# Two gate quads of the second token half: from plain filling of the second attention to Strassen quads behind the first half's

## The chip, the cores and the metric

One core of a Trainium2 chip runs the whole kernel. The metric is device microseconds of one execution; before the change the median of three runs is 2586.55 us.

## The reference, cut to what matters

One encoder layer on 2048 tokens of width 1024, in float32.

```python
h = rms_norm(x, norm_mix)
z = h @ w_in        # q_A 512 | k_A 128 | v_A 128 | q_B 512 | k_B 512 | v_B 512 | gate_A 1024 | gate_B 1024
y_a = windowed_gqa(q_a, k_a, v_a, sink)          # |t - s| <= 128
y_b = neighborhood_attn(q_b, k_b, v_b, rpb)      # on the 32 x 64 token grid
gates = sigmoid(concat([g_a, g_b]) + b_gate)
merged = gates[..., :1024] * (y_a @ w_proj_a) + gates[..., 1024:] * (y_b @ w_proj_b)
x = x + merged @ w_out
h2 = rms_norm(x, norm_mlp)
x = x + square(relu(h2 @ w_up)) @ w_down
out = rms_norm(x, norm_final)
```

The change concerns `z = h @ w_in` alone, and of it the 1024 columns of gate_B for tokens 1024 to 2047.

## The kernel before, in words

Every product of float32 operands is made of three matmuls: an operand is split into a high part (a cast on ScalarE, `L314`) and a low part (what the cast left, a subtraction on VectorE, `L315`), and high x high, high x low and low x high are added up in PSUM (`mm3s`, L318 to L320, or `mm3`, L205 to L207).

Tokens are four blocks of 512. The first two blocks ("the first half") are projected in **quads**. A quad is a 2 x 2 Strassen-Winograd product: two blocks of 256 columns of `w_in`, two halves of the 1024 features, two token blocks. Seven products instead of eight, in the order 1, 2, 5, 6, 7, 4, 3 (`ORDER`); each has two tiles of 128 columns, each tile 4 chunks x 3 matmuls of 128x512. A quad has a left operand for each product, made from its weights (`zraw`, two loads of 1 MB, then sums on VectorE and splits into `zwhl`, a ring of three buffers), and a right operand, a **page** of h (`zh1` to `zh7`, high and low part), which is the same for all quads. Three PSUM banks for each tile column, x, z and y, take products 1 and 2, 5 and 3, and 6, 7 and 4; between products VectorE adds what a bank holds to a partial result (`zc`, L309), and the next product into that bank waits for that. There are nine quads: one for k_A and v_A, one for q_A, three for q_B, k_B, v_B, four for the gates. I count them from one: the sixth to the ninth make the gates. Gate results go to DRAM (`zg`) by SP's queue.

The third and fourth block ("the second half") are normalised during the sixth and seventh quad and written to DRAM as `h1d`. Behind the ninth quad they are loaded again, multiplied by the gain `g_mix` and split into `hT` (`h_pages`, L703 to L716). Their projection is **plain**: slices of 128 columns (`raw`, 512 KB, split into `whl` by ScalarE and POOL), 8 chunks x 3 matmuls for each of the two blocks. These tiles are the filling of the two attentions: `fill` gives one chunk, three matmuls, at a time, and `plain(upto)` takes as many as a formula says between an attention's scores, transposes and products. The first attention takes 192 chunks (`PLAIN`). The second has 32 units of 4 steps, and spreads over its 128 steps the chunks up to 520 (`last_plain + PLAIN`). The last 24 are issued at its end. The order of the tiles is: k_A, v_A, q_A, then k_B, q_B, v_B by turns, then the 16 gate tiles (`gate_tile`).

In a step of the second attention (`turn`, `score`, `plain`, `product`) TensorE transposes the weights of one unit into `pt`, scores a unit two further on into `s`, does filling, and multiplies the transposes of the step before with `vb`. VectorE adds the bias to scores (L1114), ScalarE takes the exponential (L1122), POOL scales (L1127) and makes bias tiles from `braw` (L1064).

Source order is a priority; a scheduler that knows a time model of the chip sets the order on each engine, and an engine then works its instructions in that order.

Of the kernel before, what the change touches and what calls it, by code (L numbers as in the profile page):

```python
# [8 lines left out]
F32 = mybir.dt.float32  # L9
F32R = mybir.dt.float32r  # L10
AF = mybir.ActivationFunctionType
ALU = mybir.AluOpType
# [3 lines left out]
D = 1024  # L16
# [79 lines left out]
def encoder_layer(ctx, tc, x, norm_mix, w_in, b_gate, sink, rpb, w_pa, w_pb, w_out,  # L96
# [295 lines left out]
    def in_weights(c, w):  # L392

        return [row_half(c, w, p) for p in range(2)]
# [83 lines left out]
    def is_v(col):  # L478
        return col == O_VA or O_VB <= col < O_GA

    def in_result(col, b, src, in_psum):

        if col < O_VB and col != O_VA:
            for dst, t in qk_parts(col, b, src, in_e()):
                SY.dma_start(dst, t)
            return
        if in_psum:
            t = in_e()[:, 0] if is_v(col) else in_c()
            A.copy(t, src)
            src = t  # L490
        if is_v(col):
            for dst, t in v_parts(col, b, src, zbank(tpool, 2), in_v2[-1]()):
                SY.dma_start(dst, t)
        else:
            f = (col - O_GA) // P
            SY.dma_start(zg[b][0][f // 8, (f % 8) * P : (f % 8 + 1) * P, :], src)

    def in_quad(c, w, lf, right, ybanks=ypool, zbanks=zpool):

# [160 lines left out]
            G.tensor_scalar(tb, tb, 8.0, 1.0, ALU.mult, ALU.mult)  # L660
            SY.dma_start(tabs[n], tb)

    for q in range(2, len(QUADS)):
        if q == 5:
            s_v.close()
            in_v2.pop()
# [5 lines left out]
        if q + 1 < len(QUADS):  # L672
            ws = in_weights(*QUADS[q + 1])
        if q in (5, 6):

            b = q - 3
# [4 lines left out]
        for n, _ in enumerate(quad2 if q == 2 else in_quad(*QUADS[q], iter(lf), right)):  # L681
# [1158 lines left out]
```

## Time and profile before

| what | value |
|---|---|
| runs | 2582.53, 2586.55, 2589.74 us |
| profiled execution, span from first to last instruction | 2581.8 us |
| TensorE busy, granted clock | 2557.6 us (99%), 0.999 |
| VectorE, ScalarE, POOL busy | 1607.1, 1235.7, 404.0 us |
| ninth quad | 318.84 to 357.66 us of the span |
| first attention | from there to about 609 us |
| second attention | about 609 to 993 us |

A matmul's busy time overlaps with the next one's, so TensorE's 99% says that it hardly ever waits, not that it is at its peak. The profiled execution's own time is its span; nothing else is known of it, and it lies 4.75 us under the median of the runs.

### The profile page before, as it was taken

What the parts mean: (1) busy time and instruction counts of PE and PEld (TensorE: products, weight loads), DVE (VectorE), ACT (ScalarE), POOL (GpSimd) and SP (SyncE); (2) the same over time, 40 slices, a digit from 0 to 9 for tenths busy, and PEclk for the clock granted to TensorE, in tenths of its full rate; (3) what the DMA queues carried; (4) which work ended last, traced back from release to release, by engine and by line L of the source; (5) the groups of instructions that cost most, each with busy time, mean ns of one, the idle gap of its engine ahead of it and who ended that gap; (6) DMA issues with size and microseconds to landing.
All of it is one profiled execution on the core that took longest, in us unless ns stands there. A gap on an engine that the chain in (4) does not pass through costs nothing.

```text
span 2581.8 us, 34876 instructions
## 1 busy us (share of the span) xinstructions
PE 2557.6 (99%) x12200; PEld 2142.3 (83%) x12200; DVE 1607.1 (62%) x2617; ACT 1235.7 (48%) x2265; POOL 404.0 (16%) x630
## 2 busy tenths in 40 slices
PE   8999999999999999999999999999999999999999
PEld 6888888888888888888888888888888888888887
DVE  8866657765544445566578767866665535554766
ACT  5334357775555555443335554554454322323454
POOL 1001126665555440000000000100000000000010
PEclk9999999999999999999999999999999999999999
DMA  5657496577867647675357656844428835444555
GB/s 183 204 159 208 131 270 167 128 197 188 221 198 203 186 131 238 221 220 179 124 170 241 231 210 209 305 162 166 148 110 311 280 102 184 142 154 160 187 195 172
DMA packets 354128, 490.41 MB, mean 190 GB/s; under 512 B 28808, under 2 KB 188808, under 8 KB 351776
## 3 DMA queue, kind: packets, MB, share of 16 engines
q1 hardware_dynamic: 346896, 471.14, 58.5%
q10 hardware_dynamic: 7056, 17.04, 1.8%
q8 instruction: 96, 1.57, 0.3%
q14 instruction: 80, 0.66, 0.1%
HBM read 328.64 MB, written 159.45 MB: 189 GB/s over the span
## 4 chain that ended last, share of the span: by engine, by line
PE 89%; DVE 3%; DMA 3%; ACT 1%; issue 1%; POOL 1%; SPq 1%; POOLq 0%; ACTq 0%; DVEq 0%
PE b L318 15%; PE b L320 15%; PE b L319 15%; PE mm L207 5%; PE mm L205 5%; PE mm L206 5%; PE zb L320 3%; PE zb L318 3%; PE zb L319 3%; PE pt L205 2%; PE pt L206 2%; PE pt L207 2%; PE av L1159 2%; PE pt L1138 2%; PE s L1107 2%; PE av L920 1%
## 5 line engine op out<-in xcount | busy, mean ns | idle before, releaser
L319 PE MATMUL b<-dwh,dah 128*128 128x512 f32 x896 | 348.5, 389 | 0.0
L320 PE MATMUL b<-dwh,dah 128*128 128x512 f32 x896 | 347.6, 389 | 0.0
L318 PE MATMUL b<-dwh,dah 128*128 128x512 f32 x896 | 339.6, 389 | 0.0
L314 ACT CAST dah<-da 128x1024 fp32r<-128x1024 f32 (+1 forms) x128 | 120.9, 945 | 368.2 <-PE b L320 242.7
L315 DVE TENSOR_TENSOR dah<-da,dah 128x1024 fp32r<-128x1024 f32 (+1 forms) x128 | 139.5, 1090 | 223.7 <-ACT dah L314 220.7
L319 PE MATMUL b<-ubh,uwhlb 128*128 128x512 f32 x592 | 230.3, 389 | 0.0
L318 PE MATMUL b<-ubh,uwhlb 128*128 128x512 f32 x592 | 230.2, 389 | 0.0
L320 PE MATMUL b<-ubh,uwhlb 128*128 128x512 f32 x592 | 229.2, 389 | 0.0
L205 PE MATMUL mm<-hT,whl 128*128 128x512 f32 x544 | 218.4, 402 | 0.0
L207 PE MATMUL mm<-hT,whl 128*128 128x512 f32 x544 | 213.6, 393 | 0.0
L206 PE MATMUL mm<-hT,whl 128*128 128x512 f32 x544 | 213.1, 392 | 0.0
L319 PEld LDWEIGHTS b<-dwh,dah 128*128 128x128 f32 x896 | 168.2, 188 | 34.9
L320 PEld LDWEIGHTS b<-dwh,dah 128*128 128x128 f32 x896 | 168.2, 188 | 34.9
L318 PEld LDWEIGHTS b<-dwh,dah 128*128 128x128 f32 x896 | 168.2, 188 | 34.9
L318 PE MATMUL zb<-zh,zwhl 128*128 128x512 f32 x476 | 186.7, 394 | 5.2 <-DVE zh L542 1.6
L319 PE MATMUL zb<-zh,zwhl 128*128 128x512 f32 x476 | 186.3, 391 | 0.0
L320 PE MATMUL zb<-zh,zwhl 128*128 128x512 f32 x476 | 183.6, 392 | 0.3 <-DVE zwhl L315 0.3
L309 DVE TENSOR_TENSOR uc<-b,uc 128x512 f32<-128x512 f32 x160 | 109.1, 689 | 103.1 <-PE b L320 102.0
L1710 POOL TENSOR_TENSOR st<-st,power 128x1 f32<-128x1 f32 x16 | 13.3, 841 | 925.1 <-DVE st L1709 925.1
L318 PEld LDWEIGHTS b<-ubh,uwhlb 128*128 128x128 f32 x592 | 111.1, 188 | 23.4 <-issue 0.4
L319 PEld LDWEIGHTS b<-ubh,uwhlb 128*128 128x128 f32 x592 | 111.1, 188 | 23.2
L320 PEld LDWEIGHTS b<-ubh,uwhlb 128*128 128x128 f32 x592 | 111.1, 188 | 23.1
(272 smaller groups left out, 5883.8 us busy)
## 6 DMA issues: line engine op xcount, KB each, us to landing
at<-uc SPq DMA_DIRECT2D x224, 256.0 KB
da<-at SPq DMA_DIRECT2D x96, 512.0 KB
dw<-in_w_down_dram SPq DMA_DIRECT2D x160, 256.0 KB
uraw<-in_w_up_dram SPq DMA_DIRECT2D x32, 1024.0 KB
raw<-in_w_in_dram SPq DMA_DIRECT2D x34, 512.0 KB
zraw<-in_w_in_dram SPq DMA_DIRECT2D x16, 1024.0 KB
z<-zg SPq DMA_DIRECT2D x64, 256.0 KB
zg<-zc SPq DMA_DIRECT2D x32, 256.0 KB
```

What stands on the lines that cost most here:

```text
L205: PE.matmul(ps, lh, rh, start=first, stop=False)
L206: PE.matmul(ps, lh, rl, start=False, stop=False)
L207: return PE.matmul(ps, ll, rh, start=False, stop=last).ins
L309: return eng.tensor_tensor(out=out, in0=a, in1=b, op=op).ins
L314: casts.append(A.copy(hi, src).ins)
L315: return eng.tensor_tensor(out=lo, in0=src, in1=hi.bitcast(F32), op=ALU.subtract).ins
L318: PE.matmul(ps, lh, rh, start=first, stop=False, skip_group_check=True)
L319: PE.matmul(ps, lh, rl, start=False, stop=False, skip_group_check=True)
L320: PE.matmul(ps, ll, rh, start=False, stop=last, skip_group_check=True)
L1107: ins = PE.matmul(ps[:, :n], self.q[:, i, :], kv[:, z, B_R0[i] // 4 : (B_R0[i] + B_NR[i]) // 4, 4 * B_C0[j] : 4 * (B_C0[j] + w)], start=z ...
L1138: ins = PE.transpose(pt[:kp, at + (i - i0) * P : at + (i - i0 + 1) * P], self.s[i][:, rr : rr + kp], ident).ins
L1159: ins = PE.matmul(po[:, i0 * P : (i0 + ni) * P], self.v[:kp, c, :], src[:kp, o : o + ni * P], start=pair == x == z == 0, stop=(c == 7 and ...
```

## The change

The third and fourth gate quad (the 1024 columns of gate_B) are made for the second half too, as Strassen quads ten and eleven, behind the ninth. Their pages replace those of the first half in the same buffers (`late_page`): while the ninth quad runs, each page is built as soon as its product there is over, from `h1d`. Pages 1, 2 and 3 are blocks: two loads into the low part's place, then the gain by ScalarE (high part) and by VectorE (low part, `SCALAR_TENSOR_TENSOR` L680). Pages 5 and 7 are differences of two blocks, pages 6 and 4 those of a block and an earlier page (its high and low part, one after the other); they are loaded by halves of 512 KB into `xin`, a ring of three. The eight gate tiles of these columns leave the filling, so that 8 gate tiles are left, and `last_plain` becomes 25 x 8 chunks in place of 41 x 8: the second attention spreads 200 chunks over its 128 steps, before 328.

```diff
@@ in_result, a gate result's place
-            SY.dma_start(zg[b][0][f // 8, (f % 8) * P : (f % 8 + 1) * P, :], src)
+            SY.dma_start(zg[first_block[0] + b][0][f // 8, (f % 8) * P : (f % 8 + 1) * P, :], src)
...
-    for q in range(2, len(QUADS)):
+    LATE = QUADS[7:]
+
+    def late_page(n):
+
+        hi, lo = in_page[n](), in_page[n]()
+        j, p = {1: (0, 0), 2: (0, 1), 3: (1, 1), 5: (1, 0), 6: (1, 1), 7: (1, 1), 4: (0, 1)}[n]
+        gains = [g_mix[:, p * 4 + k : p * 4 + k + 1] for k in range(4)]
...
+        def parts(src, h, l, at):
+            for k in range(2):
+                A.activation(h[:, k], src[:, k], AF.Copy, scale=gains[at + k])
+                V.scalar_tensor_tensor(out=l[:, k], in0=src[:, k], scalar=gains[at + k], in1=h[:, k].bitcast(F32),
+                                       op0=ALU.mult, op1=ALU.subtract)
+
+        def half_page(z, j, p):
+            t = T(xp, [P, D], F32, "xin", 3).rearrange("p (k c) -> p k c", k=2)
+            SY.dma_start(t, rows(j, p, z))
+            return t
+
+        if n < 4:
+            for z in range(2):
+                SY.dma_start(halves(lo)[z].bitcast(F32), rows(j, p, z))
+        for z, (h, l) in enumerate(zip(halves(hi), halves(lo))):
+            if n < 4:
+                parts(l.bitcast(F32), h, l, 2 * z)
+                continue
+            a = half_page(z, j, p)
+            if n == 5:
+                b = half_page(z, 0, 0)
+                add(V, a, a, b, ALU.subtract)
+                parts(a, h, l, 2 * z)
+                continue
+            for k in range(2):
+                A.activation(a[:, k], a[:, k], AF.Copy, scale=gains[2 * z + k])
+            if n == 7:
+                b = half_page(z, 1, 0)
+                for k in range(2):
+                    A.activation(b[:, k], b[:, k], AF.Copy, scale=g_mix[:, 2 * z + k : 2 * z + k + 1])
+                add(V, a, a, b, ALU.subtract)
+            else:
+                for t in late[{6: 5, 4: 6}[n]]:
+                    add(V, a, a, halves(t)[z].bitcast(F32), ALU.subtract)
+            split(a, h, l, V)
+        late[n] = hi, lo
+
+    late = {}
+    plan = [(c, w, 0) for c, w in QUADS] + [(c, w, 2) for c, w in LATE]
+    for q in range(2, len(plan)):
...
+        first_block[0] = plan[q][2]
+        if q == len(QUADS):
+            right = late
+        for n, _ in enumerate(quad2 if q == 2 else in_quad(*plan[q][:2], iter(lf), right)):
+            if q == len(QUADS) - 1:
+                late_page(ORDER[n])
...
-    dense += [gate_tile(f, (2, 3)) for f in range(16)]
+    GATES = [f for f in range(16) if all(not c <= O_GA + f * P < c + 2 * w for c, w in LATE)]
+    dense += [gate_tile(f, (2, 3)) for f in GATES]
...
-    scored, begin, SCORE, last_plain = 0, given, 0.4, 41 * KC
+    scored, begin, SCORE, last_plain = 0, given, 0.4, (9 + 2 * len(GATES)) * KC
```

What it moves is seen at three places. The first is VectorE in the ninth quad, from the split of product 6's weights to the addition of the second tile's product 6 (`zc<-zb,zc`). Before, with the page work for the first attention (`hT`) between:

```order
L315 TENSOR_TENSOR zwhl_2616<-zS_2614,zwhl_2616 128x1024
L714 SCALAR_TENSOR_TENSOR hT_2937<-raw_2938,g_mix,hT_2936 128x512 x2
L714 SCALAR_TENSOR_TENSOR hT_2937<-raw_2944,g_mix,hT_2936 128x512 x2
L315 TENSOR_TENSOR zwhl_2619<-zraw_2394,zwhl_2619 128x1024
L714 SCALAR_TENSOR_TENSOR hT_2951<-raw_2952,g_mix,hT_2950 128x512 x2
L714 SCALAR_TENSOR_TENSOR hT_2951<-raw_2958,g_mix,hT_2950 128x512 x2
L309 TENSOR_TENSOR zc_2728<-zb_2715,zc_2642 128x512
L315 TENSOR_TENSOR zwhl_2622<-zraw_2396,zwhl_2622 128x1024
L182 TENSOR_TENSOR whl_3011<-raw_3009,whl_3011 128x1024
L309 TENSOR_TENSOR zc_2743<-zb_2730,zc_2657 128x512
```

The same place now, with pages 1, 5, 6 (in `xin`) and 2 of the second half:

```order
L315 TENSOR_TENSOR zwhl_2616<-zS_2614,zwhl_2616 128x1024
L309 TENSOR_TENSOR zS_2965<-zraw_2631,zraw_2629 128x1024
L680 SCALAR_TENSOR_TENSOR zh_279_2664<-zh_279_2664,g_mix,zh_278_2663 128x512 x4
L315 TENSOR_TENSOR zwhl_2619<-zraw_2394,zwhl_2619 128x1024
L680 SCALAR_TENSOR_TENSOR zh_285_2744<-xin_2745,g_mix,zh_284_2743 128x512 x2
L309 TENSOR_TENSOR xin_2795<-xin_2795,zh_284_2743 128x1024
L680 SCALAR_TENSOR_TENSOR zh_285_2744<-xin_2754,g_mix,zh_284_2743 128x512 x2
L309 TENSOR_TENSOR zc_2776<-zb_2763,zc_2646 128x512
L309 TENSOR_TENSOR xin_2795<-xin_2795,zh_285_2744 128x1024
L315 TENSOR_TENSOR zwhl_2622<-zraw_2396,zwhl_2622 128x1024
L680 SCALAR_TENSOR_TENSOR zh_283_2706<-zh_283_2706,g_mix,zh_282_2705 128x512 x2
L309 TENSOR_TENSOR zc_2791<-zb_2778,zc_2661 128x512
```

Between the two additions now stand a subtraction, a split and a gain pair, before two splits; ahead of the first stands page 5, which needs product 5 to be over.

The second place is SP's queue at the start of the ninth quad, from the last gate writes of the eighth on. Before, the loads for the first attention come behind them:

```order
L496 DMA zg_100<-zc_2512 128x512
L710 DMA raw_2938<-h1d_97 128x2x512
L710 DMA raw_2944<-h1d_97 128x2x512
L710 DMA raw_2952<-h1d_97 128x2x512
L496 DMA zg_99<-zc_2671 128x512
```

Now pages 1 and 2 (`zh`), the next weights (`zraw`) and the halves of pages 6 and 7 (`xin`):

```order
L498 DMA zg_100<-zc_2512 128x512
L690 DMA zh_279_2664<-h1d_97 128x2x512 x2
L498 DMA zg_99<-zc_2687 128x512
L690 DMA zh_283_2706<-h1d_97 128x2x512 x2
L498 DMA zg_99<-zc_2702 128x512
L552 DMA zraw_2980<-in_w_in_dram 128x4x512
L685 DMA xin_2803<-h1d_98 128x2x512
L685 DMA xin_2845<-h1d_98 128x2x512
L552 DMA zraw_2982<-in_w_in_dram 128x4x512
L685 DMA xin_2849<-h1d_98 128x2x512
```

Each of these waits in its place for a buffer to come free, and what follows waits with it.

The third place is TensorE in the second attention, one step from a score (`s`) to the products (`av`) that follow it. Before, two chunks of filling stand there, three in other steps:

```order
L1107 MATMUL s_10270<-kb_1137_9456,qb_1236_10130 128x384 x2
L205 MATMUL mm_10239<-hT_3016,whl_9917 128x512
L206 MATMUL mm_10239<-hT_3017,whl_9917 128x512
L207 MATMUL mm_10239<-hT_3016,whl_9917 128x512
L205 MATMUL mm_10239<-hT_3030,whl_9917 128x512
L206 MATMUL mm_10239<-hT_3031,whl_9917 128x512
L207 MATMUL mm_10239<-hT_3030,whl_9917 128x512
L1159 MATMUL av_666_10184<-phb_10220,vb_1202_9893 128x256
```

Now one chunk, two in other steps:

```order
L1166 MATMUL s_10366<-kb_1180_9709,qb_1254_10185 128x512 x2
L205 MATMUL mm_10371<-hT_3602,whl_9905 128x512
L206 MATMUL mm_10371<-hT_3603,whl_9905 128x512
L207 MATMUL mm_10371<-hT_3602,whl_9905 128x512
L1218 MATMUL av_664_10352<-phb_10334,vb_1242_10098 128x256
```

A third or more of the filling between a score and the products is gone. At the end of the ninth quad TensorE's order also has four matmuls of the tenth's product 1 between products 7 and 4.

More of the change, by code (lines that the diff above doesn't have):

```diff
@@ L479, in is_v @@
         return col == O_VA or O_VB <= col < O_GA
+    first_block = [0]
     def in_result(col, b, src, in_psum):
@@ L661, in bias_tables, with rows @@
             SY.dma_start(tabs[n], tb)
-    for q in range(2, len(QUADS)):
+    LATE = QUADS[7:]
[3 more added lines that the diff above has]
+        gains = [g_mix[:, p * 4 + k : p * 4 + k + 1] for k in range(4)]
+        def rows(j, p, z):
+            r = p * BT + z * 256
+            return h1d[j][r : r + 256, :].rearrange("(k p) t -> p k t", p=P)
+        def parts(src, h, l, at):
[35 more added lines that the diff above has]
+    for q in range(2, len(plan)):
         if q == 5:
@@ L671, in encoder_layer @@
         lf = list(in_left(ws, 256, (1, 2) if q == 2 else ()))
-        if q + 1 < len(QUADS):
-            ws = in_weights(*QUADS[q + 1])
+        if q + 1 < len(plan):
+            ws = in_weights(*plan[q + 1][:2])
         if q in (5, 6):
@@ L680, in encoder_layer @@
         ops2.extend(lf if q == 2 else ())
-        for n, _ in enumerate(quad2 if q == 2 else in_quad(*QUADS[q], iter(lf), right)):
+        first_block[0] = plan[q][2]
[4 more added lines that the diff above has]
+                late_page(ORDER[n])
             if q == 6 and n == 0:
```

## The prediction

> **What bounds the kernel now.** I read the page first, then the busy times of the stages, then the timeline and the waits where the change acts.
>
> ```profile
> PE 2557.6 (99%) x12200; PEld 2142.3 (83%) x12200; DVE 1607.1 (62%) x2617; ACT 1235.7 (48%) x2265; POOL 404.0 (16%) x630
> ...
> L205 PE MATMUL mm<-hT,whl 128*128 128x512 f32 x544 | 218.4, 402 | 0.0
> ...
> L318 PE MATMUL zb<-zh,zwhl 128*128 128x512 f32 x476 | 186.7, 394 | 5.2 <-DVE zh L542 1.6
> ```
>
> TensorE is the bound over the whole span, so a matmul less is time less, unless TensorE then waits. A matmul's own 390 to 400 ns are no price, since matmuls overlap; the price is the step from start to start. The stages (the eighth quad, the ninth, the first attention, the second):
>
> ```profile
> 281.00:319.00 38.00, 38.00 (x169) 31.49 (x168) 20.39 (x23) 9.52 (x11) 4.96 (x6) 1.00 0.27 86
> 319.00:357.50 38.50, 38.02 (x169) 31.11 (x167) 25.72 (x34) 19.48 (x27) 3.01 (x26) 1.00 0.75 229
> 357.50:609.00 251.50, 249.50 (x1482) 216.88 (x1480) 167.43 (x490) 178.52 (x506) 156.42 (x322) 1.00 0.65 175
> 609.00:993.00 384.00, 383.01 (x2218) 337.05 (x2219) 178.94 (x448) 216.75 (x505) 188.56 (x204) 1.00 0.69 190
> ```
>
> Columns: stretch, its length, busy time of PE, PEld, DVE, ACT, POOL, granted clock, DMA share, GB/s. TensorE idles 0, 0.5, 2.0 and 1.0 us in them. In quads VectorE does the rest of the work (20.4 of 38 us), in the second attention ScalarE (56%).
>
> The profiled span, 2581.8 us, is 4.75 us under the median of 2586.55 and just under the fastest of the three runs (2582.53). Everything below is a difference inside this span, and is put on the median.
>
> **The change, part by part.**
>
> *Matmuls taken away.* Eight gate tiles leave the filling: 8 x 2 blocks x 8 chunks x 3 = 384 matmuls. Their step there is read from nine filling matmuls between a score and a product:
>
> ```profile
> 783.78 0.39 PE L205 MATMUL mm<-hT,whl 128*128 128x512 f32 x1
> ...
> 785.83 0.28 PE L1159 MATMUL av<-phb,vb 128*128 128x256 f32 x1
> ```
>
> 2.05 us for nine, 0.228 each: 384 x 0.228 = 87.5 us less in the second attention.
>
> *Matmuls added.* Two quads of 7 products x 2 tiles x 4 chunks x 3 = 168 matmuls. The rows are the ninth quad's start and the starts of its product 6 (twelve matmuls for each of two tiles), that product's second tile, product 7, its second tile, and product 4:
>
> ```profile
> 318.84 0.39 PE L318 MATMUL zb<-zh,zwhl 128*128 128x512 f32 x1
> ...
> 335.16 0.39 PE L318 MATMUL zb<-zh,zwhl 128*128 128x512 f32 x1
> 337.88 0.39 PE L318 MATMUL zb<-zh,zwhl 128*128 128x512 f32 x1
> 340.60 0.39 PE L318 MATMUL zb<-zh,zwhl 128*128 128x512 f32 x1
> 343.32 0.39 PE L318 MATMUL zb<-zh,zwhl 128*128 128x512 f32 x1
> 346.68 0.47 PE L318 MATMUL zb<-zh,zwhl 128*128 128x512 f32 x1 [0.47 <-DVE zc L309]
> ```
>
> Twelve take 2.72 us, 0.2267 each: a quad takes 38.1 us, two take 76.2. Net of both: -11.3 us.
>
> *Pages of the second token half.* This is new vector work in front of TensorE, and the last row above already shows its danger: product 4 started 0.64 us late (346.68 for 343.32 + 2.72), because its bank was still to be read by a VectorE addition that stood behind page work. VectorE's rows there, from the last addition of the eighth quad on:
>
> ```profile
> 319.69 0.68 DVE L309 TENSOR_TENSOR zc<-zb,zc 128x512 f32<-128x512 f32 x1
> ...
> 335.55 2.74 DVE L714 SCALAR_TENSOR_TENSOR hT<-raw,g_mix,hT 128x512 fp32r<-128x512 f32 x4
> 338.20 0.69 DVE L309 TENSOR_TENSOR zc<-zb,zc 128x512 f32<-128x512 f32 x1
> 338.80 1.22 DVE L315 TENSOR_TENSOR zwhl<-zraw,zwhl 128x1024 fp32r<-128x1024 f32 x1
> 339.93 1.22 DVE L182 TENSOR_TENSOR whl<-raw,whl 128x1024 fp32r<-128x1024 f32 x1
> ...
> 344.52 1.41 DVE L714 SCALAR_TENSOR_TENSOR hT<-raw,g_mix,hT 128x512 fp32r<-128x512 f32 x2
> 345.84 0.69 DVE L309 TENSOR_TENSOR zc<-zb,zc 128x512 f32<-128x512 f32 x1
> 346.44 0.75 DVE L714 SCALAR_TENSOR_TENSOR hT<-raw,g_mix,hT 128x512 fp32r<-128x512 f32 x1
> ```
>
> From start to start a 128x1024 operation costs 1.14 us (338.80 to 339.93), a 128x512 addition 0.60, a pair with the gain 1.32. The seven pages need 16 gain operations (10.6 us) and 18 of 128x1024 (20.5 us; two of them stand in the eighth quad): 31 us of VectorE. ScalarE gets 32 activations of 128x512 (0.64, by the row of four in 2.58 below) and 6 casts of 1.05: 27 us, which its 9.5 us in a quad leave room for. VectorE has 17.6 us free in a quad, so it must borrow from the tenth quad too. I follow the order of the new program with these steps, the ninth quad starting at 318.84 as now:
> - Page 5 can be written when product 5 has been read, at 335.16. ScalarE (0.65) and VectorE's pair, subtraction and second pair end at 339.95; the addition that frees product 6's first bank ends at 340.6, when product 7 wants it: 0.2 us.
> - A subtraction, a weight split and page 2's first pair (3.6 us) stand ahead of the addition for the second bank: it ends at 344.75, TensorE was there at 343.5: 1.35 us.
> - Four matmuls of the tenth quad's product 1 now stand ahead of product 4. Their weights are cast when product 7 gives its buffer back (its second tile now ends at 344.9 + 2.7 = 347.6), 1.05 us and two handovers: 1.35 us.
> - Up to the additions after product 6 of the tenth quad VectorE has 33 operations of 1024, 16 with the gain and 10 additions, 54 us, from 320.3 on, and its own waits (for freed pages, loads, casts), 8 to 10.5 us as I step through them: the end is at 382.5 to 385. TensorE is there at 318.84 + 38.1 + 21.8 (four products) + 2.9 (the waits above) = 381.6: 1.0 to 3.4 us.
>
> The sum is 3.9 to 6.3 us; the two ends are loads that land in 3 or in 5.1 us. The row that bounds the load: a 512 KB load issued at 333.48 was waited for until 338.57; one issued at 332.15 was used unwaited by the row of 334.75.
>
> ```profile
> 332.15 0.36 SPq L710 DMA_DIRECT2D raw<-h1d  x1
> 333.48 0.38 SPq L192 DMA_DIRECT2D raw<-in_w_in_dram  x1
> ...
> 334.75 2.58 ACT L713 ACTIVATE hT<-raw,g_mix 128x512 fp32r<-128x512 f32 x4
> 337.24 1.04 ACT L314 CAST zwhl<-zraw 128x1024 fp32r<-128x1024 f32 x1
> 338.57 1.05 ACT L181 CAST whl<-raw 128x1024 fp32r<-128x1024 f32 x1 [0.29 <-DMA raw<-in_w_in_dram]
> ```
>
> I take +5. From below the bound is 0 (all hidden, 17.6 us free in each quad); from above 31 - 17.6 = 13.5 us, if only the ninth quad's room served. The 0.64 us of today comes from the page work for the first attention, which follows the last quad in either kernel, and stays. The Trainium skill, "DMA: Bandwidth & Descriptors", section "Bandwidth", measures 6.15 us for a load of 1 MB; by that, an estimate, page 2 would be whole about 0.7 us later than I have it and the sum that much worse.
>
> *DMA and queues.* 18 loads of 512 KB for pages, four of 1 MB for weights, and 16 gate writes of 256 KB that SP now issues (the ACT queue did). SP passes them in order: behind page 2's load stand gate writes and the next weights, and one weight load waits there for its buffer until about 347, with a page 7 load behind it. That one is used some 6 us after it lands, so it costs nothing unless the landing slips by that much. The stretch 281 to 319 moves 86 GB/s, so the engines have room.
>
> *The second attention with half its filling.* It shrinks from 384 to about 296.5 us, each of its 128 steps from 3.0 to 2.3 us. ScalarE loses 8 casts of 1.05 and 16 copies of 0.58, POOL 8 splits of 2.40: their busy shares become 67%, VectorE's 60%, POOL's 57%. The first attention runs at 71%, 67% and 62% and idles TensorE 2.0 us in 251.5. At that rate 296.5 us would idle 2.4 instead of 1.0: +1.4 at most by this row, 0 at least; I take +0.9. The upper bound is from the one load that came late:
>
> ```profile
> 653.99 3.06 POOL L1064 TENSOR_TENSOR biass<-braw,masks 128x288 f32<-128x288 f32 x3 [13.56 <-DMA braw<-tab]
> ...
> 657.59 0.88 PE L1138 MATMUL pt<-ident,sb 128*96 128x128 f32 x3 [0.20 <-POOL sb L1127]
> ```
>
> POOL stood 13.56 us, scaling the scores stood behind it, and TensorE lost 0.2 us there. Scores are made five steps ahead of their transposes, 15 us now and 11.6 then: the same lateness would cost 3.4 us more, twice that for two such loads, +7.
>
> *Sum.* -11.3 + 5 + 0.9 = -5.4 us: 2586.55 - 5.4 = 2581.2 us.
>
> **Rivals.**
>
> 1. *The pages hide wholly.* VectorE has 17.6 us free in each quad and TensorE's order could absorb the rest. Against it speaks the 0.64 us that 13 us of such work cost already. Then -11.3 + 0.9, 2576.2 us.
>
> 2. *A stall trips the clock.* Here TensorE idled 1.57 and 0.34 us within 3 us, and then ran eight matmuls in 3.5 us at a granted clock of 0.53 (the third column from the end of the stretch):
>
> ```profile
> 52.24 0.47 PE L318 MATMUL zb<-zh,zwhl 128*128 128x512 f32 x1 [1.57 <-DVE zh L542]
> ...
> 53.27 0.79 PE L320 MATMUL zb<-zh,zwhl 128*128 128x512 f32 x1 [0.34 <-DVE zwhl L315]
> ```
>
> ```profile
> 53.00:56.50 3.50, 3.23 (x8) 2.55 (x9) 3.50 (x5) 0.29 (x1) 0.00 (x0) 0.53 0.00 0
> ```
>
> Nearly half of 3.5 us is lost, 1.7 us a time. The waits above of 1.35 us lie 4 us apart, near that; two trips give 2584.6 us. The Trainium skill, "TensorE: Matmul & The Clock Gate", Part 1, says that the clock halves after an idle window of about 3.4 us. By that rule none of these waits would trip it and the sum stays; this trace disagrees, with 1.9 us of idleness.
>
> 3. *Slower: the DMA engines bind the second attention's first half.* The loads of keys, queries, values and bias come per step, and steps get 23% shorter, while the q, k, v filling of the first 16 units is still there.
>
> ```profile
> 609.00:660.00 51.00, 50.01 (x284) 43.28 (x285) 26.22 (x63) 28.91 (x66) 25.05 (x27) 1.00 0.86 221
> 660.00:710.00 50.00, 50.00 (x296) 44.20 (x295) 26.45 (x64) 29.46 (x68) 27.40 (x32) 1.00 0.89 238
> ...
> 640.00:660.00 20.00, 19.67 (x111) 16.90 (x110) 9.19 (x25) 11.37 (x29) 6.44 (x9) 1.00 0.80 170
> ```
>
> By tile sizes 16 units move some 24.6 MB and six q, k, v tiles 9.4 MB, 34 MB in 148 us: 230 GB/s. Full engines would give 221/0.86 = 257 or 267 GB/s, so it fits; at the rate of 640 to 660 (170/0.80 = 212) it takes 160 us, 12 us more: 2592 us. It turns the sign from 220 GB/s downward (34 MB in 154 us).
>
> That fewer matmuls were not issued is no rival: two quads of 168 against 384 is a count.
>
> **How the numbers follow.** The forecast (2579 to 2584) gets 0.43, hidden pages (2574 to 2579) 0.33, clock trips or the upper ends of both stalls (2584 to 2588) 0.15, the DMA case 0.09. About 0.3%, 7.8 us, is what a measurement of this kernel can tell from no change: faster than 2578.8 are the hidden pages and a little of the forecast, 0.36; slower than 2594.3 is the far half of the DMA case with longer stalls, 0.06; the rest 0.58. The range of 8 in 10 reaches from 2574 (-12.5: pages hidden and the waits of the attention gone) to 2590.
>
> **What would show it.** Right: 48 matmuls fewer; the second attention near 296 us with TensorE idle under 3 us; two quads more of 38 us, in which TensorE waits 4 to 6 us in all, for zc additions (L309) and for zwhl casts, at product 7 and ahead of product 4. Wrong: TensorE idle under 2 us in the ninth and tenth quad; or POOL waiting for braw and TensorE for POOL in the second attention; or a granted clock under 1.0 near 345 to 385 us. The largest doubt is the tenth quad, where VectorE's lateness is a sum of many handovers that no row of before shows.

## The result and the profile after

The changed kernel takes 2602.16 us (median of 4 runs, 2598.18 to 2604.14) against 2585.91 for the kernel before: a ratio of 1.0063, interval 1.0048 to 1.0077. It is slower by 16 us; 2581.2 was forecast. The profiled execution, the fastest of the four, has a span of 2596.4 us, 14.6 more than that of before.

The engines' line of the page shows the count of the forecast, 48 matmuls fewer, and TensorE at 98%:

```profile
PE 2554.7 (98%) x12152; PEld 2138.5 (82%) x12152; DVE 1676.8 (65%) x2693; ACT 1262.5 (49%) x2301; POOL 384.8 (15%) x622
```

The stages after (eighth, ninth, tenth, eleventh quad; first attention; second; the stretch behind it; the rest), in the columns of the prediction's windows (length, busy PE, PEld, DVE, ACT, POOL, granted clock, DMA share, GB/s):

```profile
280.50:322.50 42.00, 39.94 (x169) 32.63 (x168) 23.43 (x25) 10.64 (x13) 4.59 (x6) 0.96 0.57 191
322.50:363.50 41.00, 38.76 (x170) 31.34 (x169) 35.01 (x40) 23.59 (x32) 0.00 (x0) 1.00 0.56 198
363.50:405.40 41.90, 39.98 (x170) 32.61 (x169) 32.40 (x36) 19.40 (x26) 0.00 (x0) 0.96 0.34 121
405.40:445.00 39.60, 38.33 (x170) 31.43 (x169) 25.98 (x34) 19.48 (x27) 3.41 (x27) 1.00 0.73 233
445.00:696.60 251.60, 249.15 (x1480) 216.60 (x1479) 167.52 (x489) 178.49 (x506) 156.11 (x321) 1.00 0.65 174
696.60:1007.80 311.20, 301.52 (x1844) 268.42 (x1845) 178.20 (x448) 198.69 (x479) 169.34 (x196) 0.99 0.77 207
1007.80:1021.60 13.80, 11.04 (x51) 9.07 (x50) 3.91 (x5) 6.13 (x11) 0.00 (x0) 1.00 0.47 143
1021.60:2596.40 1574.80, 1567.93 (x6914) 1297.35 (x6913) 999.64 (x1336) 679.16 (x1021) 34.72 (x33) 1.00 0.57 194
```

The account by starts of stages in the two traces:

| stage | before | after | count alone | excess |
|---|---|---|---|---|
| up to the first attention's filling | 357.7 | 445.0 (+87.3) | +76.2 | +11.1 |
| first attention | 251.3 | 251.6 (+0.3) | 0 | +0.3 |
| second attention and the filling behind it | 397.2 | 325.0 (-72.2) | -87.5 | +15.3 |
| the rest | 1575.6 | 1574.8 (-0.8) | 0 | -0.8 |

The sum of the last column is 25.9; with -11.3 from the counts it gives +14.6. So the counts hold, and both stages that were given small terms (+5 and +0.9) lost far more. What TensorE waited for, first in the quads, then from the second attention on (total, times, longest; one of the five waits for `zc`, 0.5 us, lies ahead of the eighth quad):

```profile
PE zb L318 <- DVE zc L309: 6.8, 5, 2.1
PE zb L318 <- ACT zwhl L314: 1.1, 1, 1.1
...
PE pt L1197 <- POOL sb L1186: 5.7, 1, 5.7
PE mm L205 <- ACT z L1010: 2.8, 1, 2.8
PE av L1218 <- DVE plb L1205: 1.9, 5, 0.6
PE s L1166 <- DVE stb L1173: 1.7, 2, 0.9
```

The single waits, from TensorE's timeline:

```profile
288.62 0.50 PE L318 MATMUL zb<-zh,zwhl 128*128 128x512 f32 x1 [2.06 <-DVE zc L309]
348.31 0.50 PE L318 MATMUL zb<-zh,zwhl 128*128 128x512 f32 x1 [1.11 <-DVE zc L309]
352.46 0.50 PE L318 MATMUL zb<-zh,zwhl 128*128 128x512 f32 x1 [1.13 <-ACT zwhl L314]
387.32 0.47 PE L318 MATMUL zb<-zh,zwhl 128*128 128x512 f32 x1 [1.93 <-DVE zc L309]
434.00 0.47 PE L318 MATMUL zb<-zh,zwhl 128*128 128x512 f32 x1 [1.27 <-DVE zc L309]
704.98 0.50 PE L1166 MATMUL s<-kb,qb 128*128 128x512 f32 x1 [0.83 <-DVE stb L1173]
741.84 0.66 PE L1197 MATMUL pt<-ident,sb 128*96 128x128 f32 x2 [5.71 <-POOL sb L1186]
1010.86 0.50 PE L205 MATMUL mm<-hT,whl 128*128 128x512 f32 x1 [2.76 <-ACT z L1010]
```

Three of them bring half clock, at which half of TensorE's busy time is lost: 1.7 us in each of the first two rows, 2.4 in the third, where TensorE was busy for 4.76 of the 6.8 us (the third column from the end is the granted clock):

```profile
289.20:292.70 3.50, 3.50 (x10) 2.75 (x9) 3.43 (x4) 0.00 (x0) 1.60 (x2) 0.51 0.88 263
388.20:391.70 3.50, 3.50 (x10) 2.72 (x9) 1.84 (x2) 0.00 (x0) 0.00 (x0) 0.51 0.00 0
739.80:746.60 6.80, 4.76 (x16) 3.86 (x17) 0.66 (x3) 0.48 (x1) 5.80 (x10) 0.50 0.81 239
```

Taken from start to start, less the usual step, the quads' five waits cost 2.22, 1.27, 1.30, 2.09 and 1.44 us, 8.3 in all; with 3.4 us at half clock and less the 0.64 us of before that is the 11.1. From 696.6 to 1021.6 us the waits that cost over 0.34 us each sum to 13.0 (before: 0.8); with the 2.4 at half clock that is 14.6 more than before, about the 15.3 of the table.

The wait at 741.84 has its beginning on POOL:

```profile
738.34 2.97 POOL L1123 TENSOR_TENSOR biass<-braw,masks 128x288 f32<-128x288 f32 x3 [9.44 <-DMA braw<-tab]
741.28 2.10 POOL L1186 TENSOR_SCALAR sb<-sb,stb 128x288 f32<-128x288 f32 x4
```

POOL stood 9.4 us for one bias load, the scaling of the scores stood behind it, and TensorE behind that. Of the DMA engines at that time:

```profile
705.00:717.00 12.00, 10.67 (x61) 8.99 (x62) 8.10 (x20) 6.26 (x15) 4.45 (x6) 1.00 1.02 276
717.00:729.00 12.00, 12.00 (x76) 10.84 (x75) 7.71 (x20) 9.73 (x25) 8.78 (x8) 1.00 1.07 277
729.00:738.30 9.30, 7.13 (x46) 6.23 (x44) 5.65 (x13) 5.63 (x15) 0.00 (x0) 1.00 1.08 228
```

They are full (share above 1) for 33 us, at 228 to 277 GB/s. The kernel before has such a stretch at the same place, 32 us long:

```profile
619.00:629.00 10.00, 9.34 (x54) 8.22 (x54) 6.39 (x17) 5.16 (x14) 3.54 (x5) 1.00 1.04 285
629.00:640.00 11.00, 11.00 (x67) 9.80 (x66) 6.89 (x16) 7.55 (x17) 8.31 (x8) 1.00 1.06 314
640.00:651.00 11.00, 11.00 (x64) 9.64 (x63) 5.58 (x16) 6.68 (x16) 0.42 (x1) 1.00 1.08 206
```

So the engines had no room there before the change either. Steps of 3.0 us left the loads their time, and TensorE idled 0.7 us in these rows; shorter steps ask for the same loads sooner (ramp, below, tests that).

### The profile page after: what moved, and what is told of

It is laid out like the page before. It is cut to its first block, busy times and chain, and to the rows that moved or that the text cites. A ratio compares the mean times of both kernels' runs of the same rounds, so it can differ in the third digit from the quotient of the medians.

```text
span 2596.4 us, 34955 instructions
## 1 busy us (share of the span) xinstructions
PE 2554.7 (98%) x12152; PEld 2138.5 (82%) x12152; DVE 1676.8 (65%) x2693; ACT 1262.5 (49%) x2301; POOL 384.8 (15%) x622
## 4 chain that ended last, share of the span: by engine, by line
PE 83%; DVE 2%; DMA 2%; ACT 1%; issue 1%; POOL 1%; SPq 0%; POOLq 0%; DVEq 0%; ACTq 0%
PE b L318 16%; PE b L319 16%; PE b L320 16%; PE mm L205 4%; PE mm L207 4%; PE mm L206 4%; PE pt L205 2%; PE pt L206 2%; PE pt L207 2%; PE av L1218 2%; PE pt L1197 2%; PE s L1166 2%; PE av L978 1%; PE zb L318 1%; PE s L893 1%; PE zb L319 1%
## 5 line engine op out<-in xcount | busy, mean ns | idle before, releaser
L318 PE MATMUL zb<-zh,zwhl 128*128 128x512 f32 x588 | 231.9, 396 | 11.1 <-DVE zc L309 6.8
L319 PE MATMUL zb<-zh,zwhl 128*128 128x512 f32 x588 | 231.7, 394 | 0.0
L320 PE MATMUL zb<-zh,zwhl 128*128 128x512 f32 x588 | 227.0, 393 | 0.3 <-DVE zwhl L315 0.3
L205 PE MATMUL mm<-hT,whl 128*128 128x512 f32 x416 | 168.5, 405 | 2.8 <-ACT z L1010 2.8
L207 PE MATMUL mm<-hT,whl 128*128 128x512 f32 x416 | 163.8, 394 | 0.0
L206 PE MATMUL mm<-hT,whl 128*128 128x512 f32 x416 | 163.6, 393 | 0.0
L318 PEld LDWEIGHTS zb<-zh,zwhl 128*128 128x128 f32 x588 | 111.5, 190 | 38.3 <-DVE zc L309 4.9
L320 PEld LDWEIGHTS zb<-zh,zwhl 128*128 128x128 f32 x588 | 111.8, 190 | 24.4 <-DVE zwhl L315 1.0
L318 PEld LDWEIGHTS b<-ubh,uwhlb 128*128 128x128 f32 x592 | 111.2, 188 | 23.5 <-issue 0.4
```

What stands on the lines that cost most here:

```text
L205: PE.matmul(ps, lh, rh, start=first, stop=False)
L206: PE.matmul(ps, lh, rl, start=False, stop=False)
L207: return PE.matmul(ps, ll, rh, start=False, stop=last).ins
L318: PE.matmul(ps, lh, rh, start=first, stop=False, skip_group_check=True)
L319: PE.matmul(ps, lh, rl, start=False, stop=False, skip_group_check=True)
L320: PE.matmul(ps, ll, rh, start=False, stop=last, skip_group_check=True)
```

## The experiments

All ratios are against the kernel before, with a 95% interval; absolute times are medians, and the changed kernel's is 2602.16. Where a diff is given, it is against the changed kernel.

**The two halves of the change apart.** quads_added makes the late quads and keeps all 16 gate tiles in the filling:

```diff
-    GATES = [f for f in range(16) if all(...)]
+    GATES = list(range(16))
```

> The two late quads and their pages are made, and all 16 gate tiles stay in the filling as before (the eight are computed twice). Theory: the quads cost their 76.2 us of matmuls and about 11 us of waits and half clock, whatever the filling does, and the second attention takes its old length: 2586 + 87 = 2673 us, attention from first to last transposes as before (378 us). Rival (the waits in the quads come from what follows, or the attention suffers from the quads): the quads cost 77 us and the time is 2663, or the attention is longer than before by some us.

filling_halved drops the eight gate tiles and makes no late quads; gate_B of the second half is not computed, its loads take the first half's:

```diff
-    plan = [(c, w, 0) for c, w in QUADS] + [(c, w, 2) for c, w in LATE]
+    plan = [(c, w, 0) for c, w in QUADS]
-                late_page(ORDER[n])
-  SY.dma_start(g, zg[b][0][n, f * P : (f + 1) * P, :])
+  SY.dma_start(g, zg[b % 2 if n else b][0][n, f * P : (f + 1) * P, :])
```

> No late quads; the eight gate tiles are left out of the filling, and the gates of gate_B for the second half are read from the first half's place (that part is not computed). Theory: the second attention has its own loss, since its loads come in a shorter time: it saves about 73 of the 87.5 us, 2513 us, with a wait of TensorE for POOL's scaling and a half clock some 40 us behind its start. Rival (the late quads leave a backlog behind that the attention pays): it saves all 87.5, 2498 us.

Measured: 2671.74 us (1.0329, 1.0314 to 1.0344) and 2514.33 (0.9722, 0.9706 to 0.9738), that is +85.8 and -71.6. Against the counts, 76.2 and -87.5, the version with the quads loses 9.6 us and the one with the shorter attention 15.9, each alone. The rows, first the three quads from the ninth on and the second attention of quads_added, then the second attention of filling_halved:

```profile
322.20:442.20 120.00, 115.63 (x505) 94.03 (x504) 93.41 (x108) 62.50 (x85) 2.18 (x24) 1.00 0.55 184
696.50:1079.20 382.70, 382.02 (x2215) 336.44 (x2216) 178.78 (x448) 216.10 (x504) 188.44 (x204) 1.00 0.68 191
```

```profile
612.50:926.80 314.30, 304.67 (x1844) 271.03 (x1845) 178.00 (x448) 198.73 (x479) 169.27 (x196) 0.98 0.77 205
```

With its full filling the second attention idles TensorE 0.7 us even behind late quads; with half, 9.6 us and 0.98 of the clock, even without them. The loss belongs to the missing filling. The profiled run of quads_added had full clock throughout. Up to the first attention's filling it is 8.3 us above the count (442.2 - 357.7 - 76.2), which is the price of the quads' waits alone; its first attention took 3.0 us more than before (254.3 for 251.3).

**What the second attention waits for.** k_later loads the keys of the third and later heads two units later:

```diff
-            if n % 4 == 2 and n + 6 < len(units):
-                kbs[(n + 6) // 4] = load_k((n + 6) // 4)
+            if n % 4 == 0 and 0 < n and n + 4 < len(units):
+                kbs[(n + 4) // 4] = load_k((n + 4) // 4)
```

> As the changed kernel, but the keys of a head are loaded two units later (from the third head on), so that the second and third head's keys don't follow each other at the attention's start. Theory (a burst of loads fills the DMA engines and the bias rows behind it come late): the wait of 5.7 us for POOL and its half clock go, 8 to 10 us less than the changed kernel, 2592 to 2594 us. Rival (thin filling leaves waits everywhere): no change, 2602 us. Third: the burst is only moved and bites later, 2598 to 2602.

Measured: 2598.22 (1.0048, 1.0033 to 1.0063). The 5.7 us wait shrank to 1.3, but the scores' wait near 705 us grew and was followed by half clock there. keys_both also moves the second head's keys, from behind the first unit's scores to ahead of the fourth unit:

> As k_later, and the second head's keys are loaded only ahead of the fourth unit instead of behind the first unit's scores. Theory (the DMA engines are full at the start of the second attention, and what is asked for first delays the bias loads): beside the 4 us of k_later the waits of 1.05 and 1.06 us near 705 us and the half clock behind them (1.7 us) go, 2594 to 2595. Rival (the bytes are the same and the burst only moves): as k_later, 2598, with the waits elsewhere.

Measured: 2598.82 (1.0054, 1.0039 to 1.0069), no gain over k_later. The wait for bias was back, with 5.0 us of TensorE behind it:

```profile
741.26 2.97 POOL L1123 TENSOR_TENSOR biass<-braw,masks 128x288 f32<-128x288 f32 x3 [9.02 <-DMA braw<-tab]
```

The rival holds: the burst moves, its bytes stay. braw_act issues the bias loads from ScalarE instead of SP (`A.dma_start(raw, src)`):

> As the changed kernel, but the bias rows (braw) are loaded by the ACT queue and not by SP's. If the rows wait in order behind the keys in SP's queue, they land some us after their issue, POOL's wait of 9.4 us and TensorE's 5.7 go: 2593 to 2595 us. If the engines are simply full and share between queues, the rows come half as late: 2597 to 2600. If ACT's issue is late itself (its instructions wait in order): no gain, or a loss, 2602 to 2606.

Measured: 2602.64 (1.0068, 1.0053 to 1.0083), no gain. The 5.7 us wait for POOL is gone from this trace, but others came:

```profile
PE s L1166 <- DVE stb L1173: 3.4, 2, 2.5
...
PE av L1218 <- ACT phb L1204: 2.2, 3, 0.9
```

The longest, 2.5 us at 707 us, comes from an earlier bias load, for which POOL now waited 4.2 us (2.6 in the changed kernel), and 6.8 us of half clock began behind it. From 717 to 738 us the engines were as full as before (share 1.07). So another queue moved the lateness from one bias load to another and did not remove it. The Trainium skill, "DMA: Bandwidth & Descriptors", section "Issuing engines are not separate DMA queues", says that issuing from several engines saves only the issuing time; this run agrees (2602.64 against 2602.16).

ramp leaves the loads and gives them time: the first 24 steps get 18 groups of three matmuls more of the filling, the later ones as much less.

```diff
-        plain(begin + round((... * whole - scored * SCORE) / STEP))
+        lead = 18 * min((at + 1) / 24, (len(pairs) - 1 - at) / (len(pairs) - 24))
+        plain(begin + round((... * whole - scored * SCORE) / STEP + lead))
```

> The filling of the second attention is spread unevenly: its first 24 of 128 steps get 18 groups of three matmuls (12 us) more than their even share, and the other steps as much less. Theory (the loads of the first units take 12 us longer than steps of 2.3 us leave them): the POOL wait for bias of 9.4 us, TensorE's 5.9 us behind it, the half clock behind that (3.4 us) and some of the small waits near 705 to 750 go, 8 to 12 us: 2590 to 2594. Rival (ScalarE and VectorE at short steps are what binds, everywhere): the later steps, shortened to 2.2 us, wait more, and the time is 2600 or more.

Measured: 2590.39 (1.0020, 1.0010 to 1.0029), 11.8 us less. Its first 42 us, and the long stretch with the shorter steps:

```profile
696.30:738.30 42.00, 40.98 (x237) 35.62 (x238) 23.09 (x54) 23.89 (x53) 19.03 (x19) 1.00 0.96 263
...
760.00:998.90 238.90, 236.76 (x1480) 211.87 (x1478) 143.53 (x366) 161.12 (x395) 133.02 (x158) 1.00 0.78 209
```

The engines move as much, at 0.96 of their time, and TensorE idles 1.0 us; the other steps, shortened, idle 2.1 in 239. That settles the greater part of the attention's loss: it was the demand for loads at its start, not ScalarE or VectorE at short steps.

What ramp left at the end is the 2.5 us wait for `z` (L1010): ScalarE's copy that frees a bank stands behind a table load and four sigmoids of the next stage. ramp_tail leaves four groups more (`- given - 4`) for the end:

> ramp, and the second attention issues four groups of three matmuls less, which are left for the stretch behind it. Theory (the 2.7 us that TensorE waits 3 us behind the last product is a bank whose copy stands on ScalarE behind a table load, four sigmoids and casts; with the bank's end 2.7 us later its copy has passed): that wait and the half clock behind it go, 3 to 4 us less than ramp: 2586.5 to 2587.5. Rival (the copies of the stretch are late anyway): the wait comes back at the next bank, 2590.

Measured: 2592.76 (1.0034, 1.0024 to 1.0045). The end's wait and its half clock went. But in the steps, 2.7 us shorter together, TensorE waited 14 times for `plb` and `phb`, 5.6 us in all (in ramp five times, 2.1 us): here the steps themselves begin to bind. ramp_head takes four groups in (`- given + 4`):

> ramp, with four groups of three matmuls more within the second attention and so four fewer behind it: the opposite of ramp_tail, whose shorter steps only turned into waits of 0.5 to 1.2 us. Theory (from some step length on TensorE waits for VectorE in each step, so filling put there is free, and the bank that ends behind the last product now ends before it): 3 to 4 us less than ramp, 2586.5 to 2587.5. Rival (ramp's waits come from the first units' loads alone): as ramp, 2590.

Measured: 2598.34 (1.0057, 1.0037 to 1.0078), 8 us worse than ramp. The profiled run, the slowest of the four, has a wait of 5.4 us in the eighth quad, which the edit does not touch, and one of 3.1 us for weights (`whl`, ScalarE) at 1089, behind the attention, each followed by half clock. Waits for `whl` of such a size stand in no profiled run without this edit (here also 2.75 us at 1181; in best3, below, 2.57 at 1078 and 4.01 at 1171), so they seem to be its own; how it causes them stays open. Neither theory held.

**What the quads wait for.** In the eighth quad an addition to `zc` stood behind the subtraction for page 5, which stood for a load:

```profile
285.60 1.23 DVE L309 TENSOR_TENSOR xin<-xin,xin 128x1024 f32<-128x1024 f32 x1 [4.85 <-DMA xin<-h1d]
286.75 1.22 DVE L309 TENSOR_TENSOR zraw<-zraw,zS 128x1024 f32<-128x1024 f32 x1
287.88 0.69 DVE L309 TENSOR_TENSOR zc<-zb,zc 128x512 f32<-128x512 f32 x1
```

page5_later holds that subtraction until the ninth quad's first copy:

```diff
-                add(V, a, a, b, ALU.subtract)
+                with tc.issue_after(copied[0]):
+                    add(V, a, a, b, ALU.subtract)
```

> VectorE's subtraction of page 5 is held until the ninth quad's first copy, so that the addition to zc behind it no longer stands 4.85 us for a load in the eighth quad. Theory (a late load, caught on VectorE's queue, costs the wait and then a stretch of half clock): the 2.22 us wait at 288.6 and the 1.7 us lost at half clock behind it go, and the time falls from 2602.2 to about 2598.2. Rival (VectorE is short in the quads altogether, so the work only crosses into the ninth quad and is waited for there): waits in the ninth and tenth quad grow by as much, and the time stays at 2601 to 2603.

Measured: 2602.47 (1.0072, 1.0045 to 1.0099). The edit changed no engine's order in the quads and the attentions, and VectorE still stands 4.13 us for page 5's load at 285; it is the changed kernel once more, and no test of the theory. As a repeat it shows that the eighth quad's waits differ between executions: here they cost 1.50 us at 288 and 2.56 at 307, with half clock behind the second alone. pages_pool gives the subtractions of pages 5, 7, 6 and 4 to POOL (`add(G, ...)`):

> The 128x1024 subtractions that build the late pages run on POOL, 2.40 us each, instead of VectorE, 1.14. Theory (VectorE's additions to zc stand behind page work): the waits of 2.22, 1.27, 1.30, 2.09 and 1.44 us in the eighth to eleventh quad and the two half-clock stretches behind them (1.7 us each) go for the most part, 11.7 us at most; I expect 5 to 9 us, 2593 to 2597. Rival (the pages themselves are late, since each waits for the one before): TensorE then waits for page operands behind POOL, and the time is 2602 or more.

Measured: 2612.53 (1.0107, 1.0092 to 1.0122), 10 us worse. quads_fix gives POOL page 4 alone and builds the bias tables in the eleventh quad (`if q == len(plan) - 1: bias_tables()`):

> The small bias tables, whose loads and stores stand on SP ahead of page 5's second load (291 to 298 us), are built in the eleventh quad instead of the eighth, and page 4's four subtractions run on POOL (2.40 us each) instead of VectorE (1.14). Theory (what is waited for in the quads is one late addition at a time): the eighth quad's wait stays at 1 to 2.5 us but ScalarE's wait for page 5's second half goes, VectorE reaches the additions of the tenth quad's product 7 some 4 us sooner, and the 2.1 us there with the half clock behind it (1.7 us) goes: 3 to 5 us less than the changed kernel, 2597 to 2599. Rival (VectorE has no slack, page 4 on POOL comes late): TensorE waits for page 4 instead, 2602 or more.

Measured: 2606.64 (1.0079, 1.0064 to 1.0094), worse. The waits of the quads in pages_pool and then in quads_fix:

```profile
PE zb L318 <- DVE zc L309: 10.9, 7, 2.9
PE zb L320 <- DVE zwhl L315: 3.2, 2, 1.8
```

```profile
PE zb L318 <- DVE zc L309: 5.0, 4, 2.3
PE zb L320 <- DVE zwhl L315: 4.5, 1, 4.5
```

There is less work on VectorE, and there are longer waits for it. The reason is in VectorE's own operations while POOL subtracts (quads_fix, the tenth quad; POOL's row first):

```profile
369.78 12.63 POOL L309 TENSOR_TENSOR xin<-xin,zh 128x1024 f32<-128x1024 f32 x4 [72.60 <-ACT xin L702]
370.66 3.38 DVE L315 TENSOR_TENSOR zh<-xin,zh 128x1024 fp32r<-128x1024 f32 x1
373.97 3.43 DVE L309 TENSOR_TENSOR zraw<-zraw 128x1024 f32<-128x1024 f32 x1
377.32 5.64 DVE L680 SCALAR_TENSOR_TENSOR zh<-zh,g_mix,zh 128x512 fp32r<-128x512 f32 x2
382.88 1.21 DVE L315 TENSOR_TENSOR zwhl<-zS,zwhl 128x1024 fp32r<-128x1024 f32 x1
```

In the changed kernel the first two take 1.22 us each and the pair 1.41. Here this work of 3.6 us, by steps, took 12.2 (370.66 to 382.88), 8.6 more, to spare VectorE 4.6 us of subtractions; TensorE waits 4.5 us for the last row. In pages_pool the same is seen wherever such an operation starts while POOL subtracts. So POOL is not merely slower than VectorE: it slowed VectorE down.

pages_held changes the order alone. The additions behind products 6 and 7 are recorded (`added[6]`, `added[7]`), `late_page(2)` is called behind product 6 of the ninth quad and `late_page(3)` behind product 7 of the tenth, and in `late_page`:

```diff
-                V.scalar_tensor_tensor(out=l[:, k], ...)
+                with tc.issue_after(added[{2: 6, 3: 7}[n]]) if n in HELD else nullcontext():
+                    V.scalar_tensor_tensor(out=l[:, k], ...)
```

> VectorE's gain operations for page 2 are held until the ninth quad's addition behind product 6 has been issued, those for page 3 until the tenth quad's behind product 7; nothing else changes. Theory (VectorE has the time, but not in the order: page work stands ahead of additions that TensorE waits for): the 1.27 us at 348 and the 2.1 us at 387 go, with the half clock behind it (1.7 us): 2597 to 2598. Rival (VectorE is full from 350 to 387, so what is held is waited for a product later): 2601 or more, with waits for pages 2 or 3.

Measured: 2598.26 (1.0051, 1.0036 to 1.0066), 3.9 us less. The waits at 348 and 387 are gone. From the ninth quad's start to the first attention, the changed kernel and then pages_held:

```profile
322.50:445.00 122.50, 117.06 (x506) 95.37 (x505) 93.39 (x108) 62.47 (x85) 3.41 (x27) 0.99 0.54 183
```

```profile
322.80:440.80 118.00, 115.45 (x506) 93.94 (x504) 93.59 (x109) 62.63 (x85) 3.18 (x26) 1.00 0.56 190
```

The same 93.5 us of VectorE, 4.5 us sooner at the end. So for these two waits it was the order on VectorE, not its time.

**Edits together.** best1 is ramp_tail with quads_fix, best2 adds page5_later, best3 is ramp_head, pages_held and the tables in the eleventh quad, best4 is ramp, these tables and page 3 alone held.

> The edits of ramp_tail and quads_fix together. Theory (the losses lie in different stages and add): ramp's 11.8 us, the end's 3.5 us and the quads' 4 us come off 2602.2: about 2583, level with the kernel before. Rival (what one stage gains the next one loses): 2587 or more.

> best1, and page 5's first subtraction held until the ninth quad's first copy, as in page5_later. Theory (page5_later gained nothing because the late second load, behind the bias tables on SP, was then waited for at 306.8 us; the tables are gone from there): the eighth quad's wait of 2 us and the half clock behind it (1.7 us) go too: 2 to 4 us less than best1, 2579 to 2581, faster than before. Rival (page 5's work, later, delays the additions of the ninth quad): as best1 or worse.

> ramp_head, pages_held and the bias tables in the eleventh quad, together. Theory (losses of three stages, each with its own cause, add): 11.8 us of ramp, 3.5 of ramp_head, 4.5 of pages_held and 1.5 to 3 of the eighth quad off 2602.2: 2579 to 2582, faster than the kernel before. Rival (a wait that is removed turns up in the next place that VectorE serves): 2587 or more.

> ramp, the bias tables in the eleventh quad, and page 3 alone held. Theory: 11.8 us of ramp, 3.8 of page 3 and some 2 of the tables off 2602.2: 2584 to 2585, level with the kernel before. Rival: as ramp, 2590.

Measured: 2598.51 (1.0050, 1.0033 to 1.0066), 2603.11 (1.0065, 1.0044 to 1.0086), 2600.44 (1.0058, 1.0043 to 1.0073) and 2589.82 (1.0017, 1.0008 to 1.0027). best4 went as its rival said, and the others miss by 15 us and more: the harm of quads_fix and of ramp_head comes along, and in best3 and best4 a wait of 2.4 to 2.6 us of the first attention (for POOL's `ve`) was followed by half clock. best2 has best1's order on every engine, as page5_later has the changed kernel's, so their 4.6 us are the spread of such medians; the 3.9 us of k_later and of pages_held and the 4.5 of quads_fix rest on their traces, not on the times alone. The last two drop those edits: ramp, pages_held, and the first gate's sigmoids issued behind the last `z` copy (`last_exp[0] = z_copy[0]` behind the filling); best6 also builds the tables in the tenth quad.

> ramp, pages 2 and 3 held as in pages_held, the bias tables in the tenth quad, and the first gate's sigmoids issued behind the last copy of the filling instead of ahead of it. Theory (four separate losses): 11.8 us (first steps of the second attention), 3.9 (order of VectorE in the quads), some 2 (eighth quad) and 4.4 (2.7 of waiting behind the last product and 1.7 of half clock) off 2602.2: 2579 to 2582, faster than the kernel before. Rival (the tables move the first attention's 2.4 us wait for POOL along, as in best3 and best4, and the sigmoids are then waited for by the first gate): 2585 or more.

> As best6 with the bias tables where the changed kernel has them. Theory: 11.8 + 3.9 + 4.4 us off 2602.2, 2582: 2 to 4 us faster than the kernel before. Rival (late sigmoids are waited for by the first gate): 2586 or more.

Measured: 2588.61 (1.0010, 1.0000 to 1.0019) and 2589.88 (1.0015, 1.0006 to 1.0024), level with before or a little slower, not faster. The profiled run of best7 has full clock throughout and a span of 2582.0 (before: 2581.8):

```profile
322.00:440.20 118.20, 115.45 (x505) 94.15 (x504) 93.63 (x108) 62.64 (x85) 3.35 (x26) 1.00 0.57 190
...
693.30:993.60 300.30, 298.62 (x1843) 266.66 (x1844) 178.84 (x450) 198.01 (x480) 169.40 (x196) 1.00 0.79 215
993.60:1004.50 10.90, 10.90 (x52) 9.06 (x50) 2.61 (x3) 2.79 (x5) 0.00 (x0) 1.00 0.65 186
```

Its second attention with the stretch behind it takes 311.2 us, 86.0 less than before, against 87.5 by the count; TensorE idles 1.7 us there. The excess up to the first attention is still 6.3 us (440.2 - 357.7 - 76.2): waits that cost 1.20, 2.44, 1.30 and 1.61 us, the first two in the eighth quad behind VectorE and its late loads, the third for ScalarE's cast, the last behind VectorE in the eleventh quad. The first attention and the rest take 1.8 and 1.9 us more; whether the sigmoids' move costs the latter was not tried. Its other ten runs, 2586.6 to 2592.5, have a mean clock of 0.997 to 0.999: so they had half-clock stretches that the profiled run did not have.

## Why the prediction was wrong

- *The counts (-87.5 and +76.2)* were right: 48 matmuls fewer, and nearly nothing else left when the waits and half clock are taken out of the account (0.7 us of the attention's 15.3).
- *The second attention (+0.9)* is the step that failed most: 15.3 was lost there. It was sized by the first attention's rate of idleness, from shares of the whole stage, and by one late load. Some 11 us of the loss (8.8 of waits, 2.4 of half clock) lie before 750 us, where the stage's needs are not its mean: from 697 to 738 us the engines move 10.1 MB (169, 276, 277 and 228 GB/s by the windows) and are full from 705 on. The sign of being wrong that the prediction named, POOL waiting for `braw` and TensorE for POOL, is there.
- *Rival 3, the DMA engines,* was the right mechanism and had a chance of 0.09. Its size, 12 us, agrees with the 11.8 that ramp gave back by luck: it came of a rate of 212 GB/s over 16 units, and the 148 us from 696.6 on moved 227 GB/s, near the 230 that were said to fit. What did not fit was the start, where keys of two heads, bias and the first units' loads come at once. The rows that it read, of 20 to 51 us with shares of 0.80 to 0.89, mix full stretches with others and hide the 32 us above 1 of the kernel before.
- *The upper bound of +7 from a late bias load* was of the right kind: 5.7 us in one such wait, and 2.4 us of half clock with it that the bound left out.
- *Pages in the quads (+5)* measured +11.1. The walk's own waits held: 1.35, 1.35 and 1.0 to 3.4 us were 1.27, 1.30 and 2.09; 0.2 did not appear. Three things were not in it: the eighth quad's 2.22 us, where two of the moved subtractions were counted as work but not as a place that stands for a load; 1.44 us ahead of the last quad's product 4, where the 0.64 of before were to stay as they were; and 3.4 us of half clock. Work that goes into an in-order queue early brings its loads' lateness with it.
- *Rival 2, half clock,* came true in two of the quads' waits, at the 1.7 us each that it gave, and again in the attention. The pair of 1.3 us waits 4 us apart, which it named, was followed by half clock in no profiled run.
- *The end of the attention* was not in the prediction: 2.76 us for a copy behind ScalarE's sigmoids, as the filling's banks end at another place now (ramp_tail moved that place, best7 the sigmoids, and either took the wait away).
- *The rest* (first attention, what follows) moved by under 1 us, as assumed.

## What to carry to other kernels

Filling that is taken out of a stage takes away time as well as matmuls, and the loads at the stage's start need that time: look for full engines in windows of some ten microseconds there, not at the mean of the stage, and if the loads do not fit, put the remaining filling there (11.8 us here). Work that is added to an in-order engine costs by what it stands in front of and by what it stands for: hold it behind the next additions (4.5 us of the stage here) before giving it to POOL, which slowed VectorE's own operations here (10 us worse for four pages). Where the expected gain is 0.4% of the time, three waits of 2 us with half clock behind them take it all.

## What the runs showed of the hardware

- Half clock followed waits shorter than expected, and not always. In the changed kernel 2.06 and 1.93 us of idleness were followed by 3.4 us of it, and 6.8 us of it began within the wait of 5.71 us, while 2.76 us at 1010.86 were followed by none; the same wait of 2.76 us, at the same instruction, had it in k_later, braw_act, pages_held, pages_pool and quads_fix and not in page5_later. Behind the first 200 us, over all profiled runs, each wait of 2.9 us or more had it; of those between 1.8 and 2.8 us about half; shorter ones only where another lay within 2 us (0.91 and 0.91 us in page5_later, where the 0.83 and 0.89 us of the changed kernel had none). Within the kernels the stretches were 3.4 or 6.8 us long, and those of one trace begin a whole multiple of 3.413 us apart (289.3 and 388.2 us in the changed kernel: 29 times). The Trainium skill, "TensorE: Matmul & The Clock Gate", Part 1, tells of a free-running window of 3413 ns; lengths and chance agree with it. Its rule that an idle window of about 3.4 us halves the clock does not: 1.93 us sufficed.
- While POOL subtracted two tensors of the pages, every VectorE operation on two such tensors that started meanwhile took longer in quads_fix and pages_pool: 2.6 to 3.4 us for a split or sum of 1.22, and 2.3 to 2.9 us for a gain operation of 0.75. POOL's own subtractions took up to 3.4 us for 2.40. The addition to `zc`, which reads one operand from a PSUM bank, kept its 0.67 us (348.92 in pages_pool).
- With a share above 1 the DMA engines moved 206 to 314 GB/s in the kernel before and 228 to 277 in the changed one, by stretch: the share tells that they are full, the rate does not.
